# Ordering the mixers' weight copies behind the product two blocks back

## The chip, the cores and the metric

The kernel runs on one core of a Trainium2 chip. Each engine of the core (TensorE, called PE in the profile, with its weight loads as PEld; VectorE, DVE; ScalarE, ACT; GpSimd, POOL; and SyncE, SP, which here only issues transfers) works through its own list of instructions in the order in which the list was written, and semaphores hold an instruction back until what it needs is there. The metric is the time of one execution on the device, in microseconds (us).

## The reference

An input of 512 tokens of 1024 features goes through a first block (one layer) and then a second block of two layers, each of which is a feed-forward part, a hybrid mixer and another feed-forward part. The change touches the two mixers alone:

```python
for l in range(DEPTH_2):                       # 2
    x = layer_norm(DN_ALPHA * x + 0.5 * swiglu(x, ffn1_w1[l], ffn1_w3[l], ffn1_w2[l]), ...)
    y = hybrid_mixer(x, w_in[l], ...)
    x = layer_norm(DN_ALPHA * x + y, ...)
    x = layer_norm(DN_ALPHA * x + 0.5 * swiglu(x, ffn2_w1[l], ffn2_w3[l], ffn2_w2[l]), ...)

def hybrid_mixer(x, w_in, ...):
    h = split_columns(x @ w_in)
    y_a = mla_mixer(...)            # latent attention
    y_b = nsa_mixer(...)            # compressed, selected and windowed attention
    y_c = dsa_mixer(...)            # attention to the top k keys of an index score
    y_d = stick_breaking_mixer(...)
    y = concatenate([y_a, y_b, y_c, y_d]).reshape(B, S, 4, D_GROUP)
    return rms_norm_2(y, group_norm_g).reshape(B, S, D_MIX) @ w_out
```

## The kernel before

Everything is kept transposed: features on the partitions, 512 tokens along the free axis. A product of float32 values is made of three passes in the `fp32r` type: each operand is split into a high part (rounded) and a low part (the rest), and hi·hi, hi·lo and lo·hi are accumulated in PSUM. Activations are split once; the weights are split on the fly by `wstream`. It loads two blocks of weights at a time into a raw buffer `wraw` (two of them) by a transfer on SP's queue, writes the high part `whi` on ACT (`copy_a`, L363; in the output projection, whose weights are centred first, L447) and the low part `wlo` on DVE (L455, or L448 when centred) or, for the two streams named in `LO_POOL` (cq and ckv), on POOL (L367). There are three buffers each of `whi` and `wlo`, so a copy can run up to three blocks ahead of the product that reads it, and waits for PE to be done with the block that had the buffer before.

`gemm_blocks` runs a product block by block: three passes over each of the 8 pieces of the contraction (kt = 8, 24 matmuls of 512 columns) into one PSUM tile, then an epilogue `epi` that takes it out. The output projection w_out is done as four products of kt = 2, one for each group of 256 features, as the groups come ready. `gemm_m_blocks` does the token-major products (p_tok, p_sv), whose epilogue is a COPY on DVE (L1280).

What the mixer does, in order: `lead` makes four projections at once (index queries iq, misc, cmp); p_tok; the DSA index scores with p_sq, p_sk and p_sv beside them; `compress` (rows gt, with a memset on POOL, transfers on SP and a COPY on DVE each); the stick-breaking attention with p_ckv, p_cq, p_nq, p_nk and p_dq beside it; then three rounds of softmax attention (`attend`) with the pieces of w_out beside them. Rotary embeddings (`rope`: a shuffle into yc, yc times sin and the sum on DVE, hz times cos on POOL) follow several projections. The top k of the index scores is a long row of MAX8 and MATCH_REPLACE instructions on DVE, spread over the stick-breaking part. Once a group's attention is done, `group_norm` squares it on ACT, adds the halves on DVE (L1340, ss) and sums with a matmul of ones.

The order of the instructions on every engine is not written by hand: a scheduler takes the program, simulates a timeline, and emits the lists. The weight copies stand under `high_priority()`, so they are put as early as their inputs and their buffers allow. `_dep(later, earlier)` tells the scheduler that one instruction comes after another, without a semaphore of its own.

Of the kernel before, what the change touches and what calls it, by code (L numbers as in the profile page):

```python
# [13 lines left out]
AF = mybir.ActivationFunctionType  # L14
# [9 lines left out]
KT = D // 128  # L24
# [273 lines left out]
class Builder:  # L298
# [9 lines left out]
    def __init__(self, ctx, tc, A, out, dbg=None, stop=None):  # L308
        self.ctx, self.tc, self.nc, self.A, self.out = ctx, tc, tc.nc, A, out
        self.dbg = dbg or {}  # L310
        self.stop = stop
        self.n = 0
        self.set = None
        self.group, self.barrier = [], None


    def uid(self, s):
# [42 lines left out]
        return i  # L360

    def copy_a(self, out, in_):
        self.nc.scalar.activation(out, in_, AF.Copy)  # L363

    def add_p(self, out, a, b, op=ALU.add):

# [43 lines left out]
    def wstream(self, name, nhalf, F, lo_pool=False, center=False, tag=None, alt=()):  # L410

        src = self.A[name]
        nc = self.nc
        per = RAW // F
        kt = F // 128
        done = 0
        while done < nhalf:
            n = min(per, nhalf - done)  # L420
            raw = self.t("wraw", (128, RAW))
            off = done * 128 * F
            nc.sync.dma_start(raw[:, :n * F], src[off:off + n * 128 * F].rearrange("(p f) -> p f", p=128))
            if center:
                rm = self.t("rm", (128, kt))
                for k in range(kt):
                    nc.vector.reduce_sum(rm[:, k:k + 1], raw.rearrange("p (m k c) -> p k m c", k=kt, c=128)[:, k],
                                         axis=AX.XY)
                nc.vector.tensor_scalar(rm, rm, -1.0 / (128 * nhalf), None, ALU.mult)
            i = 0  # L430
            while i < n:
                t = "PT" if done + i in alt else tag
                size = 512 if t else 1024
                m = max(1, min(size // F, n - i))
                pieces = []
                for o in range(0, m * F, size):
                    r = raw[:, i * F + o:i * F + min(o + size, m * F)]
                    hi, lo = (self.t(u, (128, size), F32R)[:, :r.shape[1]] for u in ((t, t) if t else ("whi", "wlo")))
                    pieces.append((hi, lo))
                    with self.tc.high_priority():  # L440
                        if center:
                            def blk(x):
                                return x.rearrange("p (m k c) -> p m k c", k=kt, c=128)

                            for k in range(kt):
                                rk, hk = blk(r)[:, :, k], blk(hi)[:, :, k]
                                nc.scalar.activation(hk, rk, AF.Identity, bias=rm[:, k:k + 1])  # L447
                                nc.vector.scalar_tensor_tensor(blk(lo)[:, :, k], rk, rm[:, k:k + 1],  # L448
                                                               hk.bitcast(F32), ALU.add, ALU.subtract)
                        else:  # L450
                            self.copy_a(hi, r)
                            if lo_pool:
                                self.add_p(lo, r, hi.bitcast(F32), ALU.subtract)
                            else:
                                nc.vector.tensor_tensor(lo, r, hi.bitcast(F32), ALU.subtract)  # L455
                for j in range(m):
                    yield pieces if m == 1 else [tuple(x[:, j * F:(j + 1) * F] for x in pieces[0])]
                i += m
            done += n

    @staticmethod
    def cut(pieces, c=128):
# [24 lines left out]
    def gemm_blocks(self, name, nblk, xs, epi, lead=0, lo_pool=False, center=False, hold=0, st=None):  # L487

        kt = len(xs)
        st = st or self.wstream(name, nblk, kt * 128, lo_pool, center, alt=(3,) if lead > 3 else ())
        if lead:
            self.lead([(self.cut(next(st)), lambda ps, m=m: epi(m, ps)) for m in range(lead)], xs)
            yield
        for m in range(lead, nblk):
            w = self.cut(next(st))
            ps = self.p("mm")
            for k in range(kt):
                b = self.passes(ps, w, k, xs[k], slice(0, S), kt)  # L500
                if k == 0 and m >= nblk - hold:
                    self._dep(b, self.tail)
            epi(m, ps)
            yield

    def gemm_halves(self, name, xs, epi, between, center):
# [15 lines left out]
    def gemm_m_blocks(self, name, ncol, xs, epi, lo_pool=False):  # L522

        st = self.wstream(name, ncol // 256 * 2, 1024, lo_pool)
        for c in range(ncol // 256):
            w = self.cut(next(st), 256) + self.cut(next(st), 256)
            for tt in range(NT):
                ps = self.p("mm")
                o = ps[:, :256]
                cs = slice(tt * 128, tt * 128 + 128)  # L530
                for k, (hi, lo) in enumerate(w):
                    self.mm(o, xs[k][0][:, cs], hi, k == 0, False)
                    self.mm(o, xs[k][1][:, cs], hi, False, False)
                    self.mm(o, xs[k][0][:, cs], lo, False, k == KT - 1)
                epi(c, tt, o)
                if tt % 2:
                    yield

# [711 lines left out]
    def mixers(self, l, hl, xs, norm, last):  # L1250
        nc = self.nc

        def keep(res, scale=1.0, ropes=()):
            def epi(ps):
                z = self.t("hz")
                nc.scalar.activation(z, ps, AF.Copy, scale=scale)
                res.append(z)
                if ropes:
                    self.rope(z, *ropes)

            return epi

# [7 lines left out]
        for res, name, nblk, ropes, alt in ((iq, "iq", 2, [(32, whole)], ()), (misc, "misc", 1, [(64, low), (32, up)], ()),  # L1270
                                            (cmp, "cmp", 1, [(64, low)], (0,))):
            epi = keep(res, 1.0, ropes)
            jobs += [(self.cut(w), epi) for w in self.wstream(f"p_{name}_{l}", nblk, KT * 128, alt=alt)]
        self.lead(jobs, hl)
        misc = misc[0]
        tok = [self.t("hz") for _ in range(NT)]

        def epi_tok(off):
            def epi(c, tt, ps):
                nc.vector.tensor_copy(tok[tt][:, off:off + 256], ps)  # L1280
            return epi

        self.gemm_m(f"p_tok_{l}", 256, hl, epi_tok(0))
# [15 lines left out]
        def out_part(n, first, res, hold=0):  # L1299
            def epi(m, ps):  # L1300
                x = xs[m]
                if first:
                    nc.vector.scalar_tensor_tensor(x, x, DN_ALPHA, ps, ALU.mult, ALU.add)
                else:
                    nc.vector.tensor_tensor(x, x, ps, ALU.add)

            return self.gemm_blocks(f"w_out_{l}_{n}", KT, res, epi, center=True, hold=hold)

# [15 lines left out]
        interleave(last)  # L1324
        parts[1]()
        interleave(out_part(1, False, res1, HOLD))
        n = self.Norm(self, *norm)
        self.last_product(f"w_out_{l}_2", xs, res, n)
        return n
# [368 lines left out]
```

## Time and the profile before

| | us |
|---|---|
| median of 3 runs | 3313.14 |
| lowest and highest | 3311.83, 3313.3 |
| the profiled execution, its own time | 3313.87 |
| span of that execution in the trace | 3312.1 |
| PE busy | 3206.3 (97%) |
| DVE busy | 1660.5 (50%) |
| ACT busy | 1245.8 (38%) |
| POOL busy | 426.7 (13%) |

The shares are means over the whole program. In the trace, mixer 0 lies at about 1415 to 1790 us and mixer 1 at about 2540 to 2915 us; the rest is mostly dense products.

### The profile page before, as it was taken

To read this page: it belongs to the slowest core of one execution; us is meant where nothing else is said; L and a number is where in the kernel's file an instruction comes from. 1 tells how busy PE (TensorE), PEld (TensorE's weight loads), DVE (VectorE), ACT (ScalarE), POOL (GpSimd) and SP (SyncE) were. 2 spreads that over 40 slices of the span, in tenths; PEclk is the share of its full clock that TensorE was granted. 3 is DMA by queue.
4 is the path that set the end of the run, shared out by engine and by line. 5 is a ranking of instruction groups with operands and counts; after the bars stand their busy time and mean duration, and the time that the engine had idled before them with its cause. 6 is when DMAs were issued, how large, how long until landed. Compare 5 with 4: busy or idle time off the path is not lost.

```text
span 3312.1 us, 41186 instructions
## 1 busy us (share of the span) xinstructions
PE 3206.3 (97%) x16366; PEld 2622.8 (79%) x16366; DVE 1660.5 (50%) x2795; ACT 1245.8 (38%) x2229; POOL 426.7 (13%) x509
## 2 busy tenths in 40 slices
PE   8999999999999999999799999999999998999998
PEld 7798787888888888887567888888888875688887
DVE  4244444553334333468966333453336789553335
ACT  3354624442222322245465222242223445642223
POOL 0001010210000000131433000120002315320002
PEclk9999999999999999999899999999999998999999
DMA  4221222322222222222010222212222310012221
GB/s 136 80 84 68 90 89 91 108 98 93 98 95 97 89 91 100 102 74 92 30 39 27 89 90 102 102 64 102 102 91 100 98 45 26 27 59 94 102 102 64
DMA packets 53071, 275.58 MB, mean 83 GB/s; under 512 B 11136, under 2 KB 16144, under 8 KB 22416
## 3 DMA queue, kind: packets, MB, share of 16 engines
q1 hardware_dynamic: 52736, 272.83, 23.3%
q8 instruction: 129, 2.11, 0.3%
q14 instruction: 62, 0.51, 0.0%
q10 hardware_dynamic: 144, 0.12, 0.0%
HBM read 267.69 MB, written 2.10 MB: 81 GB/s over the span
## 4 chain that ended last, share of the span: by engine, by line
PE 87%; DVE 6%; ACT 3%; POOL 1%; DMA 1%; issue 1%; SPq 0%; ACTq 0%; POOLq 0%; DVEq 0%
PE mm L370 73%; PE S L370 5%; PE T L370 4%; PE O L370 3%; PE T L939 1%; DVE wlo L455 1%; POOL x L630 1%; DVE x L586 1%; DMA wraw<-ffn_w 1%; ACT whi L363 1%; DVE yc L1245 1%; DVE x L620 0%; ACT L344 0%; DVE yc L1243 0%; DVE gt L448 0%
## 5 line engine op out<-in xcount | busy, mean ns | idle before, releaser
L370 PE MATMUL mm<-ahl,whi 128*128 128x512 f32 (+1 forms) x5104 | 1550.2, 383 | 19.6 <-DVE ahl L634 7.6
L370 PEld LDWEIGHTS mm<-ahl,whi 128*128 128x128 f32 x5104 | 943.8, 189 | 214.9 <-issue 11.1
L363 ACT ACTIVATE whi<-wraw 128x1024 fp32r<-128x1024 f32 (+1 forms) x457 | 481.9, 1056 | 1497.4 <-PE mm L370 1402.5
L370 PE MATMUL mm<-ahl,wlo 128*128 128x512 f32 (+1 forms) x2552 | 971.4, 382 | 0.2
L455 DVE TENSOR_TENSOR wlo<-wraw,whi 128x1024 fp32r<-128x1024 f32 (+1 forms) x451 | 573.6, 1273 | 665.3 <-ACT whi L363 657.0
L370 PE MATMUL mm<-hz,whi 128*128 128x512 f32 x1792 | 560.2, 394 | 1.3 <-DVE x L1175 1.3
L370 PEld LDWEIGHTS mm<-ahl,wlo 128*128 128x128 f32 x2552 | 481.5, 189 | 94.6 <-DVE wlo L455 2.8
L370 PEld LDWEIGHTS mm<-hz,whi 128*128 128x128 f32 x1792 | 336.2, 188 | 81.2 <-DVE x L1175 3.0
L370 PE MATMUL mm<-hz,wlo 128*128 128x512 f32 x896 | 352.3, 394 | 0.0
L574 POOL TENSOR_TENSOR ss<-x,x 128x512 f32<-128x512 f32 x6 | 8.7, 1456 | 1564.4 <-DVE x L1175 1564.4
L370 PEld LDWEIGHTS mm<-hz,wlo 128*128 128x128 f32 x896 | 168.1, 188 | 39.8
L370 PE MATMUL mm<-whi,ahl 128*128 128x256 f32 x896 | 170.1, 289 | 7.3 <-DVE hz L1280 6.4
L1157 DVE SCALAR_TENSOR_TENSOR tA<-mm,tA 128x512 f32<-128x512 f32 x80 | 55.3, 691 | 242.9 <-PE mm L370 242.9
L370 PEld LDWEIGHTS mm<-whi,ahl 128*128 128x128 f32 x896 | 143.2, 194 | 11.8 <-DVE hz L1280 6.8
L370 PE MATMUL mm<-wlo,ahl 128*128 128x256 f32 x448 | 128.2, 287 | 1.5 <-DVE wlo L455 1.5
L1175 DVE TENSOR_TENSOR x<-x,mm 128x512 f32<-128x512 f32 x64 | 43.5, 685 | 140.4 <-PE mm L370 140.1
L363 ACT ACTIVATE hz<-tA 128x512 fp32r<-128x512 f32 (+1 forms) x124 | 76.0, 617 | 48.7 <-DVE tA L800 40.6
L374 DVE TENSOR_TENSOR hz<-tA,hz 128x512 fp32r<-128x512 f32 (+1 forms) x124 | 82.4, 669 | 20.2 <-ACT hz L363 19.7
L370 PE MATMUL O<-PT,hz 128*64 128x128 f32 (+2 forms) x776 | 87.7, 287 | 2.2 <-ACT PT L363 2.2
L363 ACT ACTIVATE PT<-T 128x128 f32<-128x128 f32 (+3 forms) x146 | 63.8, 442 | 67.3 <-PE T L939 62.7
L370 PEld LDWEIGHTS mm<-wlo,ahl 128*128 128x128 f32 x448 | 86.9, 194 | 2.6 <-DVE wlo L455 2.1
L924 DVE TENSOR_REDUCE sm<-S 128x1 f32<-128x256 f32 (+3 forms) x128 | 61.5, 488 | 42.2 <-PE S L370 30.8
(351 smaller groups left out, 3627.6 us busy)
## 6 DMA issues: line engine op xcount, KB each, us to landing
wraw<-ffn_w SPq DMA_DIRECT2D x132, 1024.0 KB, 4.8
wraw<-w_gate SPq DMA_DIRECT2D x16, 1024.0 KB, 4.8
wraw<-w_up SPq DMA_DIRECT2D x16, 1024.0 KB, 4.8
wraw<-w_dn SPq DMA_DIRECT2D x16, 1024.0 KB, 4.8
wraw<-w_br SPq DMA_DIRECT2D x8, 1024.0 KB, 4.8
wraw<-w_out SPq DMA_DIRECT2D x8, 1024.0 KB, 4.7
wraw<-w_o SPq DMA_DIRECT2D x4, 768.0 KB, 4.9
gt<-PT SPq DMA_DIRECT2D x48, 64.0 KB, 2.0
```

What stands on the lines that cost most here:

```text
L363: self.nc.scalar.activation(out, in_, AF.Copy)
L370: return self.nc.tensor.matmul(out, lhsT, rhs, start=start, stop=stop, skip_group_check=True)
L374: self.nc.vector.tensor_tensor(lo, src, hi.bitcast(F32), ALU.subtract)
L455: nc.vector.tensor_tensor(lo, r, hi.bitcast(F32), ALU.subtract)
L574: i = nc.gpsimd.tensor_tensor(s1, xs[0], xs[1], ALU.add)
L586: nc.vector.tensor_tensor(xs[d], xs[d], m0, ALU.subtract)
L630: nc.gpsimd.tensor_scalar(y, y, 1.0, be, ALU.mult, ALU.add)
L924: nc.vector.reduce_max(st[:, 0:1], ps, axis=AX.X, negate=True)
L939: nc.tensor.transpose(pt[:, j * 128:j * 128 + 128], P[:, j * 128:j * 128 + 128], self.ident)
L1157: nc.vector.scalar_tensor_tensor(s, ps, 0.5, s, ALU.mult, ALU.mult)
L1175: nc.vector.tensor_tensor(x, x, ps, ALU.add)
L1245: nc.vector.tensor_tensor(xr[r], xr[r], self.c2(f"sin{dim}")[r], ALU.mult)
```

## The change

A list `ends` is opened in each mixer after `lead`, and closed before the last piece of w_out. Every product appends the instruction of its epilogue (of the token-major products each second one). `paced` then makes the copy of a weight's high part on ACT depend on the entry two back in the list for products with kt = 8, six back for w_out. It is an ordering alone: no instruction is added or taken out, and no instruction waits for a semaphore that it didn't need anyway.

```diff
--- before.py
+++ after.py
@@ -312,6 +312,7 @@
         self.n = 0
         self.set = None
         self.group, self.barrier = [], None
+        self.ends = None
 
 
     def uid(self, s):
@@ -360,7 +361,7 @@
         return i
 
     def copy_a(self, out, in_):
-        self.nc.scalar.activation(out, in_, AF.Copy)
+        return self.nc.scalar.activation(out, in_, AF.Copy)
 
     def add_p(self, out, a, b, op=ALU.add):
 
@@ -444,11 +445,11 @@
 
                             for k in range(kt):
                                 rk, hk = blk(r)[:, :, k], blk(hi)[:, :, k]
-                                nc.scalar.activation(hk, rk, AF.Identity, bias=rm[:, k:k + 1])
+                                self.paced(nc.scalar.activation(hk, rk, AF.Identity, bias=rm[:, k:k + 1]), kt)
                                 nc.vector.scalar_tensor_tensor(blk(lo)[:, :, k], rk, rm[:, k:k + 1],
                                                                hk.bitcast(F32), ALU.add, ALU.subtract)
                         else:
-                            self.copy_a(hi, r)
+                            self.paced(self.copy_a(hi, r), kt)
                             if lo_pool:
                                 self.add_p(lo, r, hi.bitcast(F32), ALU.subtract)
                             else:
@@ -457,6 +458,12 @@
                     yield pieces if m == 1 else [tuple(x[:, j * F:(j + 1) * F] for x in pieces[0])]
                 i += m
             done += n
+
+    def paced(self, i, kt):
+
+        back = 2 if kt == KT else 6
+        if self.ends is not None and len(self.ends) >= back:
+            self._dep(i, self.ends[-back])
 
     @staticmethod
     def cut(pieces, c=128):
@@ -500,7 +507,9 @@
                 b = self.passes(ps, w, k, xs[k], slice(0, S), kt)
                 if k == 0 and m >= nblk - hold:
                     self._dep(b, self.tail)
-            epi(m, ps)
+            end = epi(m, ps)
+            if self.ends is not None:
+                self.ends.append(end)
             yield
 
     def gemm_halves(self, name, xs, epi, between, center):
@@ -532,7 +541,9 @@
                     self.mm(o, xs[k][0][:, cs], hi, k == 0, False)
                     self.mm(o, xs[k][1][:, cs], hi, False, False)
                     self.mm(o, xs[k][0][:, cs], lo, False, k == KT - 1)
-                epi(c, tt, o)
+                end = epi(c, tt, o)
+                if self.ends is not None and tt % 2:
+                    self.ends.append(end)
                 if tt % 2:
                     yield
 
@@ -1253,10 +1264,11 @@
         def keep(res, scale=1.0, ropes=()):
             def epi(ps):
                 z = self.t("hz")
-                nc.scalar.activation(z, ps, AF.Copy, scale=scale)
+                end = nc.scalar.activation(z, ps, AF.Copy, scale=scale)
                 res.append(z)
                 if ropes:
                     self.rope(z, *ropes)
+                return end
 
             return epi
 
@@ -1272,12 +1284,13 @@
             epi = keep(res, 1.0, ropes)
             jobs += [(self.cut(w), epi) for w in self.wstream(f"p_{name}_{l}", nblk, KT * 128, alt=alt)]
         self.lead(jobs, hl)
+        self.ends = []
         misc = misc[0]
         tok = [self.t("hz") for _ in range(NT)]
 
         def epi_tok(off):
             def epi(c, tt, ps):
-                nc.vector.tensor_copy(tok[tt][:, off:off + 256], ps)
+                return nc.vector.tensor_copy(tok[tt][:, off:off + 256], ps)
             return epi
 
         self.gemm_m(f"p_tok_{l}", 256, hl, epi_tok(0))
@@ -1300,9 +1313,8 @@
             def epi(m, ps):
                 x = xs[m]
                 if first:
-                    nc.vector.scalar_tensor_tensor(x, x, DN_ALPHA, ps, ALU.mult, ALU.add)
-                else:
-                    nc.vector.tensor_tensor(x, x, ps, ALU.add)
+                    return nc.vector.scalar_tensor_tensor(x, x, DN_ALPHA, ps, ALU.mult, ALU.add)
+                return nc.vector.tensor_tensor(x, x, ps, ALU.add)
 
             return self.gemm_blocks(f"w_out_{l}_{n}", KT, res, epi, center=True, hold=hold)
 
@@ -1324,6 +1336,7 @@
         interleave(last)
         parts[1]()
         interleave(out_part(1, False, res1, HOLD))
+        self.ends = None
         n = self.Norm(self, *norm)
         self.last_product(f"w_out_{l}_2", xs, res, n)
         return n
```

The lists that come out differ on all engines, in both mixers. Three places follow; line numbers of the changed kernel are up to 13 higher.

DVE in p_tok, the stretch in which the four rotary embeddings follow `lead`. The name `mm_10826` is the first PSUM tile of p_tok, which COPY hz_10812 empties; `yc` and `hz` are the rotary embeddings, `wlo_11001` the low part of p_sq's first block. Before:

```order
L455 TENSOR_TENSOR wlo_11001<-wraw_10998,whi_11000 128x1024
L1243 STREAM_SHUFFLE yc_10798<-hz_10796 128x512
L1248 TENSOR_TENSOR hz_10782<-hz_10782,yc_10784 128x512
L1243 STREAM_SHUFFLE yc_10807<-hz_10805 128x512
L1245 TENSOR_TENSOR yc_10791<-yc_10791,c_8040 128x512
L1280 COPY hz_10812<-mm_10826 128x256
L1245 TENSOR_TENSOR yc_10798<-yc_10798,c_8040 64x512 x2
L1280 COPY hz_10813<-mm_10852 128x256
```

And in the changed kernel:

```order
L1254 STREAM_SHUFFLE yc_10807<-hz_10805 128x512
L1259 TENSOR_TENSOR hz_10782<-hz_10782,yc_10784 128x512
L1256 TENSOR_TENSOR yc_10791<-yc_10791,c_8040 128x512
L1256 TENSOR_TENSOR yc_10798<-yc_10798,c_8040 64x512 x2
L1256 TENSOR_TENSOR yc_10807<-yc_10807,c_8040 64x512
L1293 COPY hz_10812<-mm_10826 128x256
L1293 COPY hz_10813<-mm_10852 128x256
```

The low part has moved from ahead of the COPY to behind it, and two multiplications of yc_10798 and one of yc_10807 have moved ahead of it.

POOL in `compress` and at the start of the stick-breaking part: the memsets of `gt` are those of compress, `wlo_11464` is the low part of p_ckv, `wlo_11531` and `wlo_11602` those of p_cq, and tA is stick-breaking. Before:

```order
L1483 AFFINE_SELECT acc_10930<-acc_10930 128x128
L367 TENSOR_TENSOR wlo_11464<-wraw_11461,whi_11463 128x1024
L1522 MEMSET gt_11355 128x272
L1483 AFFINE_SELECT acc_10930<-acc_10930 128x128
L1522 MEMSET gt_11366 128x272
L1522 MEMSET gt_11377 128x272
L1522 MEMSET gt_11388 128x272
L367 TENSOR_TENSOR wlo_11531<-wraw_11528,whi_11530 128x1024
L367 TENSOR_TENSOR wlo_11602<-wraw_11528,whi_11601 128x1024
L1483 AFFINE_SELECT acc_10930<-acc_10930 128x128
L1662 TENSOR_SCALAR tA_11505<-PT_11502 128x128
```

And in the changed kernel (from the memset of gt_11355 on):

```order
L1535 MEMSET gt_11355 128x272
L1496 AFFINE_SELECT acc_10930<-acc_10930 128x128
L1535 MEMSET gt_11366 128x272
L368 TENSOR_TENSOR wlo_11464<-wraw_11461,whi_11463 128x1024
L1535 MEMSET gt_11377 128x272
L1535 MEMSET gt_11388 128x272
L368 TENSOR_TENSOR wlo_11531<-wraw_11528,whi_11530 128x1024
L1496 AFFINE_SELECT acc_10930<-acc_10930 128x128
L1675 TENSOR_SCALAR tA_11505<-PT_11502 128x128
```

`wlo_11464` now stands behind the memset of gt_11366; `wlo_11602` no longer stands behind `wlo_11531` but thirteen rows below it, behind tA_11772. On PE, the first scores of stick-breaking (S_11494, S_11561) now stand ahead of the last eight matmuls of compress, which before came ahead of them.

DVE ahead of the norm of the stick-breaking group: `ss_12210` is the sum for which PE's matmul waits; `wlo_12721` is the low part of the first weights of w_out's second piece, `x` the centring of the residual, `yc_12107` and `hz_12105` a rotary embedding of p_dq, `hz_13483` a split for the last attention. Before:

```order
L448 SCALAR_TENSOR_TENSOR wlo_12721<-wraw_12714,rm_12716,whi_12720 128x4x128
L1243 STREAM_SHUFFLE yc_12107<-hz_12105 128x512
L399 TENSOR_TENSOR hz_13483<-hz_10796,hz_13482 64x512
L1433 COPY gt_12143<-hz_10796 32x512
L1245 TENSOR_TENSOR yc_12107<-yc_12107,c_8040 128x512
L924 TENSOR_REDUCE sm_12231<-S_12228 128x1
L924 TENSOR_REDUCE sm_12245<-S_12242 128x1
```

with four rows of x between these and the following:

```order
L1248 TENSOR_TENSOR hz_12105<-hz_12105,yc_12107 128x512
L924 TENSOR_REDUCE sm_12281<-S_12278 128x1
L1340 TENSOR_TENSOR ss_12210<-ss_12210,ss_12212 128x512
L389 TENSOR_TENSOR hz_13488<-hz_12020,hz_13488 64x512
L931 TENSOR_SCALAR sm_12231<-sm_12231 128x1
```

And in the changed kernel, ahead of and behind the same sum:

```order
L597 TENSOR_TENSOR x_5421<-x_5421,ss_12187 128x512
L430 TENSOR_SCALAR rm_13850<-rm_13850 128x2
L1446 COPY gt_12143<-hz_10796 32x512
L1254 STREAM_SHUFFLE yc_12107<-hz_12105 128x512
L935 TENSOR_REDUCE sm_12245<-S_12242 128x1
L1353 TENSOR_TENSOR ss_12210<-ss_12210,ss_12212 128x512
L935 TENSOR_REDUCE sm_12281<-S_12278 128x1
L400 TENSOR_TENSOR hz_13483<-hz_10796,hz_13482 64x512
L942 TENSOR_SCALAR sm_12231<-sm_12231 128x1
L1256 TENSOR_TENSOR yc_12107<-yc_12107,c_8040 128x512
L390 TENSOR_TENSOR hz_13488<-hz_12020,hz_13488 64x512
L935 TENSOR_REDUCE sm_12296<-S_12293 128x1
```

Ahead of the sum both parts of wlo_12721, the multiplication of yc_12107, the addition into hz_12105 and hz_13483 are gone; the last three stand behind it, wlo_12721 far behind, among the attention.

## Rows read from the trace of the kernel before

**Rows 1.** The page: busy time of PE and DVE, and the two weight copies' groups

```profile
PE 3206.3 (97%) x16366; PEld 2622.8 (79%) x16366; DVE 1660.5 (50%) x2795; ACT 1245.8 (38%) x2229; POOL 426.7 (13%) x509
...
L363 ACT ACTIVATE whi<-wraw 128x1024 fp32r<-128x1024 f32 (+1 forms) x457 | 481.9, 1056 | 1497.4 <-PE mm L370 1402.5
...
L455 DVE TENSOR_TENSOR wlo<-wraw,whi 128x1024 fp32r<-128x1024 f32 (+1 forms) x451 | 573.6, 1273 | 665.3 <-ACT whi L363 657.0
```

**Rows 2.** Busy time by window: us, PE, PEld, DVE, ACT, POOL, granted clock, DMA

```profile
1530.00:1600.00 70.00, 70.00 (x337) 50.45 (x337) 61.23 (x148) 35.25 (x75) 11.56 (x26) 0.95 0.13 47
1600.00:1655.00 55.00, 38.02 (x142) 23.48 (x140) 51.98 (x97) 23.52 (x52) 28.45 (x23) 0.81 0.05 20
...
2732.00:2787.00 55.00, 38.55 (x150) 23.01 (x149) 52.58 (x103) 27.51 (x65) 32.00 (x27) 0.81 0.06 19
```

**Rows 3.** Waits from 1430 to 1790: total us, times, longest us

```profile
ACT whi L363 <- PE mm L370: 29.7, 12, 9.8
...
ACT whi L447 <- PE mm L370: 16.3, 5, 4.8
```

**Rows 4.** Timeline in p_tok: start, us, instruction, [idle before, releaser]

```profile
1466.39 1.21 DVE L455 TENSOR_TENSOR wlo<-wraw,whi 128x1024 fp32r<-128x1024 f32 x1
...
1470.89 0.41 DVE L1280 COPY hz<-mm 128x256 f32<-128x256 f32 x1
1471.22 3.11 DVE L1245 TENSOR_TENSOR yc<-yc,c 64x512 f32<-64x512 f32 x2
...
1471.35 0.50 PE L370 MATMUL mm<-whi,ahl 128*128 128x256 f32 x2 [3.19 <-DVE hz L1280]
...
1474.82 0.68 DVE L1245 TENSOR_TENSOR yc<-yc,c 64x512 f32<-64x512 f32 x1
```

**Rows 5.** Timelines of POOL, DVE and PE at the end of compress

```profile
1517.58 5.11 POOL L367 TENSOR_TENSOR wlo<-wraw,whi 128x1024 fp32r<-128x1024 f32 x2 [1.03 <-ACT whi L363]
...
1515.62 0.75 DVE L1480 SCALAR_TENSOR_TENSOR acc<-tA,sm,acc 128x512 f32<-128x512 f32 x1
...
1516.67 0.58 DVE L1525 COPY gt<-hz 64x128 f32<-64x128 f32 x2
...
1517.86 2.63 DVE L1480 SCALAR_TENSOR_TENSOR acc<-tA,sm,acc 128x512 f32<-128x512 f32 x1
1520.41 2.70 DVE L1525 COPY gt<-hz 64x128 f32<-64x128 f32 x2
...
1523.21 1.61 PE L370 MATMUL mm<-gt,gt 128*68 128x128 f32 x8 [2.07 <-POOL wlo L367]
```

**Rows 6.** Busy time by window behind that wait

```profile
1523.50:1537.00 13.50, 13.50 (x53) 10.60 (x50) 11.52 (x42) 5.67 (x16) 1.64 (x5) 0.50 0.13 41
```

**Rows 7.** Timelines of DVE and PE ahead of the stick-breaking group's norm

```profile
1603.60 0.75 DVE L448 SCALAR_TENSOR_TENSOR wlo<-wraw,rm,whi 128x512 fp32r<-128x512 f32 x1 [2.02 <-ACT whi L447]
...
1635.47 0.75 DVE L448 SCALAR_TENSOR_TENSOR wlo<-wraw,rm,whi 128x512 fp32r<-128x512 f32 x1
...
1636.76 0.67 DVE L399 TENSOR_TENSOR hz<-hz,hz 64x512 fp32r<-64x512 f32 x1
...
1638.86 1.64 DVE L1245 TENSOR_TENSOR yc<-yc,c 128x512 f32<-128x512 f32 x1
...
1647.10 0.68 DVE L1248 TENSOR_TENSOR hz<-hz,yc 128x512 f32<-128x512 f32 x1
...
1648.86 2.04 PE L370 MATMUL mm<-ss,ones 128*128 128x512 f32 x2 [4.79 <-DVE ss L1340]
```

**Rows 8.** Timeline of PE in the first attention round

```profile
1686.11 0.66 PE L939 MATMUL T<-ident,tA 128*128 128x128 f32 x4 [1.74 <-POOL tA L934]
```

**Rows 9.** Timelines of DVE and PE: a low part of p_nq, a top-k row, the product's first matmuls

```profile
1556.03 1.23 DVE L455 TENSOR_TENSOR wlo<-wraw,whi 128x1024 fp32r<-128x1024 f32 x1 [1.01 <-ACT whi L363]
...
1567.84 0.69 DVE L1496 MAX8 m<-acc 128x8 f32<-128x512 f32 x1
...
1572.49 0.72 PE L370 MATMUL mm<-ahl,whi 128*128 128x512 f32 x2
```

## The prediction

> **What bounds the kernel now.** I read the busy shares first [rows 1]: PE works 97% of the span, so all that an ordering can give back is time in which PE stands still or runs at half its clock, or time that PE would newly lose. The groups of the two weight copies show that a copy of a high part takes 1.06 us on ACT and waits for PE nearly always (1402.5 of its 1497.4 us of idle time), and that the low part takes 1.27 us on DVE and then waits for ACT. The copies thus run as far ahead as three buffers allow and stand in front of other work while they wait for a buffer; the reader is to see that the new ordering doesn't make a copy wait for more, it puts other instructions in front of it.
>
> Then I cut the mixers into windows [rows 2]. From 1530 to 1600 PE is busy throughout and DVE for 61.23 of 70 us. From 1600 to 1655 it turns over: DVE is busy 51.98 of 55 us and PE only 38.02, at a granted clock of 0.81; the window of mixer 1 that lies 1132 us later shows the same (52.58 and 38.55). So in this window DVE's list sets the time, and ahead of it PE does. The waits of the mixer say what the copies cost the lists they stand in [rows 3]: ACT stands 29.7 us in 12 waits, and in w_out's copies 16.3 us in 5, for a buffer that PE still reads. Idle time of ACT is worth nothing by itself; it is worth something where DVE or PE waits for what stands behind.
>
> **The change, place by place (one mixer; the second has the same order).**
>
> *p_tok: a loss.* PE waits 3.19 us here for the COPY that frees its PSUM tile [rows 4]. A low part (1.21 us) leaves DVE's list ahead of the COPY, but two multiplications of yc_10798 (3.11 us for the two, beside POOL's part of the rotary embeddings) and one of yc_10807 come ahead of it. The last took 0.68 us once POOL had gone quiet. At its worst it takes half of 3.11, so that the COPY comes 3.11 + 1.55 - 1.21 = 3.45 us later; at best all three take 0.68, and it is 2.04 - 1.21 = 0.83 us. POOL's work doesn't move much, so I take the multiplications nearer the upper price, and 2.5 us.
>
> *Compress: a gain that may not show.* PE waits 2.07 us for the last eight matmuls. The row puts it down to POOL's low part; the last thing that ended before is DVE's COPY of gt, which took 2.70 us for two where the pair before took 0.58, as an accumulation took 2.63 instead of 0.75, both beside the 5.11 us in which POOL made two low parts [rows 5]. In the changed list the second of these is far behind, and PE has scores of stick-breaking to do before it needs gt, so I expect the wait to go. Behind it the granted clock is 0.50, that is 1.2 of 2.4 GHz, for 13.5 us of unbroken work [rows 6]; at full clock these take half, 6.75 us less. The bounds are 0 and 2.07 + 6.75 = 8.8 us. I take 1: what PE wins here it mostly waits out at 1600, where DVE is late, and POOL's second low part is only moved.
> The Trainium skill ("SBUF — State Buffer", "SBUF: two separate sides") says that VectorE and GpSimd share one port pair as an exclusive lock, held for a whole instruction, and that a VectorE instruction with two SBUF inputs is blocked by it. The stretched rows agree (2.63 against 0.75 us). By that rule the moved low part would block DVE again at its new place; that is a rival below.
>
> *1600 to 1655: the main gain.* PE waits 4.79 us for the sum ss of the stick-breaking group [rows 7], and in the window as a whole PE stands 17 us, while DVE has 3 us free. Ahead of the sum the changed list lacks w_out's low part in two halves (0.75 each), the multiplication of yc (1.64), the addition into hz (0.68) and a split (0.67): 4.5 us. A wait of DVE for a w_out copy (2.02 us, the first of these rows) can go too, since copies no longer stand ahead of their turn. Lower bound: no gain, if what DVE lacks then is PE's or ACT's result, and a loss of 2.3 us if the gates of NSA hold PE up, since one rotary embedding's multiplication and addition (1.64 + 0.68) now stand ahead of them. Upper bound: the 17 us that PE stands. I take 4.5, the rows taken out and nothing else. What is late next is the rotary embedding of p_dq, needed for the last attention only.
>
> *The attention rounds.* The w_out copies come later here, among the rounds, where they no longer stand in front. A wait of PE for POOL, 1.74 us [rows 8], stands behind DVE work of this kind; I take 1.7 as gone, with 0 and 4 as bounds (the short waits beside it, and the half clock behind them, make up the rest). If the moved low parts crowd DVE in the later rounds it is a loss of 1.
>
> *Weights that come too late: nothing.* A copy may now begin when the product two blocks back has ended, and needs 1.06 + 1.27 us [rows 1] and its place in DVE's list. Before, the low part of p_nq was made at 1556.03 and read first after 1572.49 [rows 9], so 16 us of lead are there, of which the low part itself takes 1.2. The changed list puts 19 rows of the top k ahead of it, at 0.69 us at most if they are like the row of that group, 13 us. What covers it is the lead alone; if that is gone, each block waits for up to a copy of each kind, 2.3 us, and for 12 waiting copies in a mixer that would be 28 us.
>
> Sum for a mixer: +2.5 - 1 - 4.5 - 1.7 = -4.7 us; for two, -9.4. On the profiled execution's 3313.87 us that is 3304.5; the median of the runs lies 0.73 lower, so 3304 us to the nearest.
>
> **Rivals.** *The clock comes back (more gain).* If compress's stall goes and PE's earlier arrival does move DVE's list, a mixer gains 8.8 instead of 1: +2.5 - 8.8 - 4.5 - 1.7 = -12.5, and two give 3288 us. For it: the half clock begins right behind that stall. Against it: DVE is 87% busy from 1530 on.
> *Nothing measurable.* The delayed COPY and late arrivals eat what DVE's list saves: for each mixer +2.5 and -1.7, and PE's 4.79 us wait only changes its name; about 3314. For it: PE's own work after 1530 leaves little to shorten.
> *The lock moves.* The low part of p_cq (2.5 us on POOL, half of 5.11) blocks DVE at its new place, in a stretch where DVE sets the time: -4.7 + 2.5 = -2.2 for a mixer, 3309.5. For it: the two stretched rows. Against it: the rows that were stretched are of other kinds than the top k which fills DVE there.
> *Slower: p_tok's COPY decides.* It comes 3.45 us later, PE's stall of 3.19 becomes 6.6, and a half clock as long as that behind compress follows (6.75 us); 1600 to 1655 gains nothing, since DVE's inputs come later by as much. +3.45 + 6.75 - 1.7 = 8.5 for a mixer, 3330 us; without the half clock 3317. It decides from the point at which the COPY's delay passes the 4.5 us that DVE's list gives back, clock included. *Slower: late weights.* If half of the 12 copies come late by 2.3 us, a mixer loses 13.8 and wins 4.7: 3331 us.
>
> **How the numbers follow.** A change of under 0.2%, 6.6 us, is about what a measurement of this kernel can't tell from none. Chances: the forecast 0.41, the clock's return 0.15, nothing 0.16, the lock 0.07, p_tok's COPY 0.12, late weights 0.09. Faster by over 0.2% are the first two, 0.56; within it the next two, 0.23; slower the last two, 0.21, though the first of these starts within. The likeliest case alone, by its bounds, is 3295 to 3310. The range takes in the clock's return with a little of its upper bounds (two mixers at -14.5: 3284) and the milder end of p_tok's COPY, 3320; beyond it lie late weights, the COPY with half clock and a full return of all idle time at 1600.
>
> **What would show it.** In the changed trace, p_tok's PE wait for the COPY should be 5 to 6.5 us instead of 3.19. The eight matmuls at compress should start without a wait, and the 13.5 us behind at a clock near 1. ss should come some 5 us sooner after the end of the top k, and PE's window there hold less idle time. No row of PE or its weight loads should wait for wlo in the mixers. The prediction fails if such waits appear, if the COPY's delay is carried through to the end of the mixer, or if DVE's idle time before 1600 grows by what its list has lost.

## The result, and the profile after

The changed kernel is slower: a median of 3335.59 us over 6 runs (3324.84 to 3338.57) against 3313.18 for the kernel before, a recorded ratio of 1.0061 with a 95% interval of 1.0050 to 1.0073 (the two medians alone give 1.0068). The forecast was 3304 us, and the range ended at 3320. Two things are to be kept apart: where the loss came from, and why six runs of one program now lie 14 us apart, when six of before lie within 2 (and the 16 to 23 of before in the groups below within 8 to 10). One execution each of `out_only` (12050.25 us), `sq_only` (8049.49) and `tok_act` (8249.82) below lasted far longer than all others and is left out of their ratios and medians here, which moves the medians by at most 1.2 us (`sq_only`'s is 3328.21 with it).

The profiled execution is the fastest of the six, 3324.84 us, with a span of 3322.8. Of the page, the lines that answer to [rows 1]:

```profile
PE 3209.3 (97%) x16362; PEld 2620.7 (79%) x16366; DVE 1659.4 (50%) x2795; ACT 1250.0 (38%) x2229; POOL 426.5 (13%) x509
...
L364 ACT ACTIVATE whi<-wraw 128x1024 fp32r<-128x1024 f32 (+1 forms) x457 | 482.2, 1057 | 1460.5 <-PE mm L371 1368.4
...
L456 DVE TENSOR_TENSOR wlo<-wraw,whi 128x1024 fp32r<-128x1024 f32 (+1 forms) x451 | 577.4, 1281 | 672.7 <-ACT whi L364 664.6
```

Busy times hardly differ, which is right for a change of order: DVE's differs by 1 us and PE's by 3. The span grew by 10.7 us, so PE stands still (span less busy time) for 113.5 us instead of 105.8: 7.7 of the 10.7 us are PE standing longer. The windows that answer to [rows 2]:

```profile
1530.00:1600.00 70.00, 70.00 (x349) 49.95 (x350) 61.01 (x153) 36.15 (x77) 14.90 (x28) 1.00 0.11 39
1600.00:1655.00 55.00, 38.60 (x140) 22.62 (x138) 50.19 (x99) 25.07 (x56) 29.13 (x22) 0.81 0.10 39
2732.00:2787.00 55.00, 37.88 (x145) 25.07 (x145) 51.19 (x92) 22.66 (x48) 26.34 (x22) 0.85 0.11 39
```

From 1600 to 1655 PE is busy 38.6 us, where it was 38.0: the gain that the forecast rested on is not there. Of the waits of [rows 3], ACT's for a buffer of whi fell from 29.7 to 12.4 us in the mixer, and its row for w_out's copies is gone from the list. The copies wait less for a buffer, as they were meant to, but PE works no more for it.

```profile
ACT whi L364 <- PE mm L371: 12.4, 4, 9.8
```

The waits of PE in mixer 0 (1400 to 1810, in us, times, longest) name what it stood for instead:

```profile
PE T L1618 <- DVE tA L1616: 7.8, 1, 7.8
PE mm L371 <- DVE hz L1293: 6.4, 1, 6.4
PE S L371 <- ACT tA L357: 3.7, 2, 3.2
...
PE S L371 <- DVE PT L1667: 2.3, 1, 2.3
...
PE mm L371 <- DVE wlo L456: 0.3, 1, 0.3
```

The second row is p_tok's COPY, 3.19 us in [rows 4]. On the timeline of DVE and PE it reads:

```profile
1467.45 5.80 DVE L1256 TENSOR_TENSOR yc<-yc,c 128x512 f32<-128x512 f32 x4
1473.18 0.74 DVE L1293 COPY hz<-mm 128x256 f32<-128x256 f32 x2
...
1473.64 0.80 PE L371 MATMUL mm<-whi,ahl 128*128 128x256 f32 x2 [6.36 <-DVE hz L1293]
```

Four multiplications take 5.80 us ahead of the COPY, and PE stands 3.17 us longer (6.36 less 3.19). Mixer 1 has the same wait of 6.36 us, so the two make 6.3 of the 7.7 us that PE stands longer. The fourth row is new: where [rows 5] had PE wait 2.07 us for the end of compress, it now waits for DVE's first tiles of stick-breaking, in both mixers:

```profile
1528.79 0.49 PE L371 MATMUL S<-PT,c 128*128 128x128 f32 x2 [2.31 <-DVE PT L1667]
...
2654.31 0.49 PE L371 MATMUL S<-PT,c 128*128 128x128 f32 x2 [2.30 <-DVE PT L1667]
```

DVE comes late to this tile for two reasons that the trace shows. It has three more rows ahead of it than before (an accumulation, a MAX8 and a MATCH_REPLACE8 with its load), and another accumulation on the way takes 2.93 us, where the one behind it takes 0.73, beside POOL's low part of p_cq's first block. Mixer 1 has the same row (2.92 us). No run parts the two reasons.

```profile
1521.24 2.93 DVE L1493 SCALAR_TENSOR_TENSOR acc<-tA,sm,acc 128x512 f32<-128x512 f32 x1
...
1521.28 2.35 POOL L368 TENSOR_TENSOR wlo<-wraw,whi 128x1024 fp32r<-128x1024 f32 x1 [2.22 <-ACT whi L364]
```

And here the two mixers part, with one order of instructions and one and the same wait. The windows behind it:

```profile
1530.50:1554.00 23.50, 23.50 (x138) 16.33 (x138) 21.99 (x77) 13.04 (x34) 4.89 (x13) 1.00 0.01 4
...
2655.00:2678.00 23.00, 23.00 (x77) 14.93 (x78) 14.97 (x54) 9.95 (x25) 4.86 (x13) 0.50 0.00 0
```

In mixer 0 the granted clock stays at 1.00, that is 2.4 GHz, and PE gets 138 matmuls done in 23.5 us; in mixer 1 it is 0.50, 1.2 GHz, and PE does 77 in 23 us, while DVE, which is fed by PE here, is busy 15 us instead of 22. The transfer that opens each mixer dates the loss. Before and after, for the first and the second mixer:

```profile
1400.03 0.33 SPq L423 DMA_DIRECT2D wraw<-p_iq  x1
...
2526.73 0.33 SPq L423 DMA_DIRECT2D wraw<-p_iq  x1
```

```profile
1400.79 0.33 SPq L424 DMA_DIRECT2D wraw<-p_iq  x1
...
2524.30 0.33 SPq L424 DMA_DIRECT2D wraw<-p_iq  x1
```

Mixer 0 and the feed-forward parts behind it take 1123.5 us instead of 1126.7, 3.2 less; from mixer 1 to the end of the span it is 798.5 instead of 785.4, 13.1 more. So in this execution the mixer whose clock holds behind the new wait is slightly faster than before, and the one whose clock falls there loses 13 us. Of these, PE stands 5.7 us longer (48.0 against 42.3, p_tok's 3.2 among them) and works 7.4 us longer, before and after:

```profile
2526.73:3312.10 785.37, 743.08 (x3924) 594.32 (x3922) 465.55 (x913) 326.45 (x679) 167.13 (x200) 0.97 0.20 70
...
2524.30:3322.80 798.50, 750.46 (x3922) 597.65 (x3922) 466.54 (x913) 328.31 (x679) 165.74 (x200) 0.96 0.20 69
```

Over the whole program the mean granted clock is 0.984 in this run, as in the profile of before, so its loss is mostly standing time. The slower runs have a lower clock besides: 0.982 in the next (3331.18 us), and 0.979 to 0.980 in the four others (3334.84 to 3338.57). That a slower run has a long half clock in both mixers is inferred from these means; only the fastest has a profile.

### The profile page after: what moved, and what is told of

The parts are those of the page before. It is cut to its first block, busy times and chain, and to the rows that moved or that the text cites. A ratio compares the mean times of both kernels' runs of the same rounds, so it can differ in the third digit from the quotient of the medians.

```text
span 3322.8 us, 41165 instructions
## 1 busy us (share of the span) xinstructions
PE 3209.3 (97%) x16362; PEld 2620.7 (79%) x16366; DVE 1659.4 (50%) x2795; ACT 1250.0 (38%) x2229; POOL 426.5 (13%) x509
## 4 chain that ended last, share of the span: by engine, by line
PE 88%; DVE 6%; ACT 2%; DMA 1%; issue 1%; POOL 1%; SPq 0%; ACTq 0%; DVEq 0%; POOLq 0%
PE mm L371 74%; PE S L371 5%; PE T L371 4%; PE O L371 3%; PE T L950 1%; DVE wlo L456 1%; POOL x L641 1%; DMA wraw<-ffn_w 1%; DVE yc L1256 1%; DVE x L597 1%; ACT whi L364 1%; DVE x L631 0%; DVE rm L428 0%; DVE yc L1254 0%; ACT L345 0%
## 5 line engine op out<-in xcount | busy, mean ns | idle before, releaser
L371 PEld LDWEIGHTS mm<-whi,ahl 128*128 128x128 f32 x896 | 143.5, 195 | 18.1 <-DVE hz L1293 13.1
```

The source lines that it names most:

```text
L371: return self.nc.tensor.matmul(out, lhsT, rhs, start=start, stop=stop, skip_group_check=True)
```

## The experiments

Eleven kernels, each timed beside runs of the kernel before on the same chip (medians of before: 3313.96, 3313.76 and 3313.47 us in the three groups, which are close enough to compare medians between groups). They differ in which copies are ordered, or in who makes one COPY.

### Which part of the ordering costs

`prod_only` leaves w_out's copies as before, `out_only` orders them alone:

```diff
-        back = 2 if kt == KT else 6
-        if self.ends is not None and len(self.ends) >= back:
+        back = 2
+        if kt == KT and self.ends is not None and len(self.ends) >= back:   # prod_only
+        back = 6
+        if kt != KT and self.ends is not None and len(self.ends) >= back:   # out_only
```

> Only the copies of products with kt = 8 are ordered; w_out's copies stand as before. Theory (the loss is PE's longer wait for p_tok's COPY and the wait at the start of stick-breaking, each with a half clock behind it): as slow as the full change, 3325 to 3340 us, with runs 10 us apart, p_tok's wait at 6.4 us and the 2.3 us wait at the first stick-breaking tile in both mixers. Rival (w_out's copies come too late among the attention rounds): 3310 to 3316 us.

Measured: 3331.96 us, ratio 1.0051 (1.0039 to 1.0064). p_tok's wait is 6.36 us, the new wait 2.31 and 2.32 us, and the half clock follows in both mixers of this profile, for some 10 us in the first and 23 in the second (3325.52 us, so a half clock in both mixers does not by itself make a run as slow as the median). The loss is in the products' copies.

> Only w_out's copies are ordered, six blocks back; the products' copies stand as before. Theory: p_tok's wait stays 3.2 us, nothing moves before the attention rounds, and the time is 3308 to 3316 us with runs within 3 us of each other. Rival (w_out's copies come too late): 3320 us or more, with waits of PE for wlo or whi in the attention rounds.

Measured: 3316.9 us, ratio 1.0005 (0.9996 to 1.0014): no difference. PE's waits from 1600 to 1660, before:

```profile
PE mm L370 <- DVE ss L1340: 4.8, 1, 4.8
PE S L370 <- ACT tA L356: 4.1, 1, 4.1
PE S L370 <- DVE gt L1433: 4.0, 1, 4.0
```

and with w_out's copies ordered:

```profile
PE S L371 <- ACT tA L357: 9.1, 2, 5.0
PE S L371 <- DVE gt L1446: 7.0, 2, 6.0
```

The wait for ss is gone, and the other two have grown from 8.1 to 16.1 us. w_out's low part no longer stands ahead of the sum, but DVE comes no sooner to the sum: ahead of some of the copies of gt that PE needs, it stands still for the transfer of w_out's next weights, in mixer 0 and as long in mixer 1.

```profile
1636.99 2.35 DVE L428 TENSOR_REDUCE rm<-wraw 128x1 f32<-128x1024 f32 x2 [2.32 <-DMA wraw<-w_out]
```

So this run shows that the ordering of w_out's copies is worth nothing, and not what an earlier sum would be worth; that is read from the trace of the full change, in the part on why the prediction was wrong.

`after_tok` opens the list only ahead of compress, so that p_sq, p_sk and p_sv are not ordered, nor the copies of p_ckv and of p_cq's first block, which are written while the list has fewer than two entries; `not_pool` orders all but the two streams whose low parts POOL makes:

```diff
         self.lead(jobs, hl)
-        self.ends = []
...
+        self.ends = []                       # after_tok
         comp = self.compress(l, cmp[0])
...
-                            self.paced(self.copy_a(hi, r), kt)
+                            i_ = self.copy_a(hi, r)
+                            if not lo_pool:  # not_pool
+                                self.paced(i_, kt)
```

> The ordering begins only ahead of compress, so p_tok, p_sq, p_sk and p_sv have the order of before, while the low part of p_cq on POOL still moves behind the first stick-breaking rows. Theory: p_tok's wait is 3.2 us again; PE's scores of stick-breaking stand behind compress as before, so the wait at the first tile of stick-breaking is gone, and the time is 3303 to 3315 us. Rival (the moved low part on POOL blocks DVE and causes the loss): 3325 us or more in spite of p_tok.

Measured: 3297.81 us, ratio 0.9951 (0.9939 to 0.9963). This is a gain of 16 us out of the same idea, over two mixers. PE's matmuls of compress now run through, with no wait at the last eight, and the clock holds behind them. The row of PE, and the windows behind it in mixers 0 and 1:

```profile
1517.96 3.76 PE L371 MATMUL mm<-gt,gt 128*68 128x128 f32 x32
```

```profile
1518.00:1536.00 18.00, 17.06 (x114) 13.09 (x113) 17.95 (x57) 12.59 (x34) 4.77 (x11) 1.00 0.12 38
2634.00:2652.00 18.00, 17.06 (x109) 12.56 (x107) 17.95 (x60) 12.76 (x35) 4.39 (x11) 1.00 0.12 38
```

> All copies are ordered but those of the two streams whose low parts POOL makes (ckv and cq), so POOL's list is that of before, while p_tok's COPY stands late as in the full change. Theory: p_tok's wait is 6.4 us; that alone costs 3.2 us and 1.7 us of half clock in a mixer, so at least 3320 us. Rival (POOL's moved low part causes the loss): 3310 to 3316 us.

Measured: 3321.44 us, ratio 1.0025 (1.0016 to 1.0034). p_tok's wait is 6.36 us, and the time is still above before's. The rival, that POOL's moved low part is the loss, falls in this form, since the run before has p_cq's second one moved and gains. But this run is 14 us under the full change, and the intervals are apart: beside the late COPY, more than half of the loss goes when the copies of p_ckv and p_cq keep their order. PE's wait for the first tile of stick-breaking is 0.32 us here instead of 2.31 (with 1.50 at the end of compress, and half clock for 6.8 us behind).

### The COPY, and what stands behind it

`sq_only` orders the copies of p_sq alone, `from_sq` opens the list behind p_tok, `tok_act` is the full change with p_tok's COPY on ACT, and `after_tok_act` has that COPY in `after_tok`:

```diff
-                            self.paced(self.copy_a(hi, r), kt)
+                            i_ = self.copy_a(hi, r)
+                            if name.startswith("p_sq"):          # sq_only, and none in w_out
+                                self.paced(i_, kt)
...
         self.gemm_m(f"p_tok_{l}", 256, hl, epi_tok(0))
+        self.ends = []                                           # from_sq
...
+                if off == 0:                                     # tok_act, after_tok_act
+                    return nc.scalar.activation(tok[tt][:, off:off + 256], ps, AF.Copy)
                 return nc.vector.tensor_copy(tok[tt][:, off:off + 256], ps)
```

> Only the copies of p_sq are ordered, which leaves p_tok's COPY as late as in the full change and all that follows compress much as before. Theory (the late COPY is the loss): p_tok's wait is 6.4 us in both mixers, PE comes late to the first tiles of stick-breaking, and the time is 3318 to 3335 us. Rival (the loss comes from the ordering of the products behind p_sq): 3311 to 3317 us.

Measured: 3327.1 us, ratio 1.0043 (1.0030 to 1.0056). p_tok's wait is 6.36 us. One product's two copies, ordered, make more than half of the loss. They also bring 11 more rows of DVE (its short MATCH_VALUE_LOAD not counted), mostly top k, ahead of the first tile of stick-breaking, for which PE then waits 3.04 us, so this run doesn't part the COPY from that backlog.

> The ordering begins behind p_tok: the COPY stands as before, p_sk and all that follows is ordered, and PE's scores of stick-breaking stand ahead of the end of compress as in the full change. Theory: no wait of over 1.5 us between p_tok and 1600 us, no half clock there, 3293 to 3305 us. Rival (the scores ahead of compress cause the new wait and its half clock): 3320 us or more.

Measured: 3310.76 us, ratio 0.9991 (0.9983 to 1.0000): between the two forecasts, 25 us under the full change and 13 us over `after_tok`. The COPY's place is worth most of the loss, but the order of the copies of p_sk, p_sv, p_ckv and p_cq's first block, which `after_tok` leaves as before, takes back most of what that run had won. The timeline of POOL, DVE and PE shows the old trouble in the new order:

```profile
1517.24 2.35 POOL L368 TENSOR_TENSOR wlo<-wraw,whi 128x1024 fp32r<-128x1024 f32 x1 [1.28 <-ACT whi L364]
...
1517.32 2.95 DVE L1538 COPY gt<-hz 64x128 f32<-64x128 f32 x2
...
1520.37 1.06 PE L371 MATMUL mm<-gt,gt 128*68 128x128 f32 x8 [1.75 <-DVE gt L1538]
```

POOL's one low part now begins just ahead of the two copies of gt and they take 2.95 us instead of 0.58; PE waits for them, and the clock is halved behind, in both mixers:

```profile
1522.00:1532.00 10.00, 9.63 (x41) 8.11 (x41) 9.26 (x27) 5.16 (x16) 0.59 (x2) 0.50 0.13 30
2645.00:2655.00 10.00, 9.30 (x39) 7.49 (x38) 8.99 (x26) 4.96 (x15) 0.59 (x2) 0.50 0.11 25
```

In `after_tok` a low part of the same length stands at nearly the same time, but DVE has an accumulation beside it, which PE doesn't wait for:

```profile
1517.18 2.35 POOL L368 TENSOR_TENSOR wlo<-wraw,whi 128x1024 fp32r<-128x1024 f32 x1 [1.03 <-ACT whi L364]
...
1517.46 2.63 DVE L1493 SCALAR_TENSOR_TENSOR acc<-tA,sm,acc 128x512 f32<-128x512 f32 x1
1520.01 0.55 DVE L1538 COPY gt<-hz 64x128 f32<-64x128 f32 x2
```

The meeting alone does not make PE wait so long: in `cq_only` below the two copies take 2.71 us beside POOL's low part, and PE, which has 24 other matmuls of compress to do meanwhile, waits 0.18 us.

> The full change, but p_tok's COPY is made by ACT instead of DVE, so that it doesn't stand behind the rotary embeddings (same work on another engine, about 0.5 us each). Theory: p_tok's wait falls below 1.5 us, the first stick-breaking tile comes without a wait, 3285 to 3302 us. Rival (the loss lies behind p_tok and not in the COPY): 3320 us or more with the 2.3 us wait still there.

Measured: 3306.24 us, ratio 0.9979 (0.9970 to 0.9988), 29 us under the full change for p_tok's COPY made by ACT. PE's wait for that COPY, now at p_sq's first matmul, is 1.97 us (expected under 1.5), and the wait at stick-breaking's first tile is gone. The time is above the expected 3302; one wait of 1.75 us for gt, as in `from_sq`, with a half clock behind, is what the trace shows for it.

> The ordering that begins ahead of compress, with p_tok's COPY on ACT. Theory: the 3.2 us wait of the kernel before in p_tok and the 3.4 us of half clock behind it go in both mixers, so up to 4.9 us for each under the run with the ordering from compress on: 3287 to 3296 us. Rival (what PE wins in p_tok it waits out at the top k): 3296 to 3300 us.

Measured: 3295.20 us, ratio 0.9945 (0.9933 to 0.9957). PE's wait for p_tok's COPY is down to 1.3 us, but the interval overlaps with that of `after_tok`: a difference between the two isn't shown.

### One move at a time

`cq_only` and `sq_cq` order the copies of p_cq alone, and of p_sq and p_cq; `after_tok_prod` is `after_tok` without w_out:

```diff
-                            self.paced(self.copy_a(hi, r), kt)
+                            i_ = self.copy_a(hi, r)
+                            if name.startswith("p_cq"):            # cq_only
+                            if name[:4] in ("p_sq", "p_cq"):       # sq_cq
+                                self.paced(i_, kt)
...
-                                self.paced(nc.scalar.activation(hk, rk, AF.Identity, bias=rm[:, k:k + 1]), kt)
+                                nc.scalar.activation(hk, rk, AF.Identity, bias=rm[:, k:k + 1])   # all three
```

> Only the copies of p_cq are ordered: POOL's second low part moves behind the first rows of stick-breaking, p_tok and the attention rounds keep the order of before. Theory (the gain of the ordering from compress on is this one move: two copies of gt no longer blocked, no wait at the last eight matmuls of compress, no half clock behind): about 7 us in a mixer up to the end of stick-breaking, 3297 to 3303 us. Rival (that gain is eaten by DVE at 1600, and what was gained comes from w_out's copies): 3310 to 3314 us.

Measured: 3306.83 us, ratio 0.9985 (0.9976 to 0.9994). DVE has the same rows ahead of the first tiles of stick-breaking and of its norm; POOL's second low part and its high part on ACT have moved. It is worth 6.6 us by the medians (5 by the ratio), half of what the theory had: the wait of 2.07 us is 0.18, but a half clock still follows (0.52 from 1526 to 1533), and the 4.8 us wait for ss stays.

> Only the copies of p_sq and p_cq are ordered: p_tok's late COPY and POOL's move together, nothing else. Theory (the late COPY brings PE's compress up against DVE's backlog, so that the move can no longer save the clock): the wait and half clock at the start of stick-breaking stay, 3318 to 3332 us, little better than p_sq alone (3328.21). Rival (the two simply add): p_sq alone less the gain of p_cq alone, about 3314 us if that is 14 us.

Measured: 3323.74 us, ratio 1.0032 (1.0020 to 1.0043). With the COPY late, a wait of 3.02 us for the first tile of stick-breaking and the half clock stay. But by the ratios p_sq alone costs 0.43% and p_cq alone gives 0.15%, and the sum of the two, 0.28%, lies within the interval of this run; the claim that the late COPY makes the move worthless isn't borne out, only that the move doesn't make up for it.

> The ordering from compress on without w_out's copies. Theory (w_out's copies are worth nothing, as they were alone): 3295 to 3300 us, as with them (3297.81). Rival (they are worth the 1.5 us of low parts ahead of the norm and the waits of the attention rounds, 3 us in a mixer, once PE's clock is up): 3302 to 3306 us.

Measured: 3296.20 us, ratio 0.9952 (0.9939 to 0.9964), the same as with w_out's copies. Their ordering is worth nothing, here as alone.

## Why the prediction was wrong

**p_tok: right.** The step took 2.5 us between 0.83 and 3.45; the wait grew by 3.17. The step did not count the clock behind the longer wait, and little is lost by that. The half clock lasts 6.8 us instead of 3.4, but much of it falls on the wait itself: PE works 3.46 us at half clock in mixer 0 and 5.00 in mixer 1, where it worked 3.40 before. (The 1.7 us that the expectation of `not_pool` adds for it are too much for the same reason.) After, in both mixers, and before:

```profile
1470.30:1477.10 6.80, 3.46 (x16) 3.46 (x17) 6.75 (x12) 1.27 (x4) 1.61 (x2) 0.50 0.22 55
...
2596.70:2603.50 6.80, 5.00 (x23) 5.00 (x24) 6.74 (x15) 2.77 (x6) 0.14 (x1) 0.50 0.24 58
```

```profile
1472.40:1475.80 3.40, 3.40 (x18) 3.40 (x17) 3.32 (x5) 0.21 (x1) 1.38 (x1) 0.50 0.32 77
```

**Compress: the step that failed.** It said "PE has scores of stick-breaking to do before it needs gt, so I expect the wait to go", and took the clock behind it at no more than a gain that is waited out later. In the changed kernel the wait did go from compress, and stood again some matmuls on, at the tiles whose scores PE had done early: DVE was behind, with three more rows ahead of the first tile and an accumulation stretched from 0.73 to 2.93 us. The step asked what PE needed and did not ask what DVE would still have to do when PE came there. In place of a gain of 1 us stood a wait of 2.3 us, and in mixer 1 the 23 us at half clock behind it, where before had some 13.5. Its sizing failed too: `after_tok` shows that the ordering from compress on, met by an unchanged start, is worth about 8 us in a mixer (16 for two), near the step's upper bound of 8.8, of which POOL's move alone makes about 3 (`cq_only`); the step had 1. The argument that an early PE only waits at 1600 was wrong, since DVE in stick-breaking is fed by PE: at half clock DVE was busy 14.97 us of 23, at full clock 21.99 of 23.5.

**1600 to 1655: wrong, and the largest term of the sum.** The 4.5 us were read off the rows ahead of one sum. In mixer 0 that sum did come 6 us sooner, counted from the transfer that opens the mixer, and PE has no wait for it (before, then after):

```profile
1648.04 0.68 DVE L1340 TENSOR_TENSOR ss<-ss,ss 128x512 f32<-128x512 f32 x1
...
1642.74 0.68 DVE L1353 TENSOR_TENSOR ss<-ss,ss 128x512 f32<-128x512 f32 x1
```

PE is busy 38.60 us of the window all the same, where it was 38.02: other results of DVE and ACT took the sum's place, NSA's gated scores first (7.81 us for tA in mixer 0). The lower bound had named these gates, and the rival "nothing measurable" had said that PE's wait only changes its name. The wait of [rows 7] was one of several of nearly the same length, and the list behind it was not followed. In mixer 1 the sum came 13 us later than before, counted likewise.

**The attention rounds: not shown.** The 1.74 us of [rows 8] are gone in mixer 0, and a wait of 1.50 stands ten us later; w_out's ordering, to which the step ascribed them, is worth nothing in two pairs of runs.

**Late weights: right.** PE waits 0.3 us for wlo at the start of p_tok in each mixer, as it did before, and nowhere else in the mixers; the lead [rows 9] was enough.

**The rivals.** "p_tok's COPY decides" came nearest, with 3317 us without the half clock and 3330 with it, at a chance of 0.12. It placed the half clock behind p_tok and the reason for no gain at 1600 in DVE's inputs; measured, the half clock that the change adds lies mostly behind stick-breaking's first tile, in mixer 1. That the lock moves was given 0.07, and 2.5 us in a mixer; in the full change an accumulation is stretched by 2.2 us, but by p_cq's first low part and not by the second, which the rival had in mind, and in `from_sq` that part meets the copies of gt. (The rival's 3309.5 lacks the 0.73 us that the other sums take off; it would be 3308.7.)

**A mixer that came near the forecast by luck.** Mixer 0 of the profiled execution is 3.2 us shorter, where the sum had 4.7. The gains at 1600 and in the attention rounds, 6.2 us of that sum, did not come; what came instead is full clock behind compress, where before had 13.5 us at half clock [rows 6].

By differences of medians: ordering the copies from p_sq to p_cq's first block turns the 16 us gain of `after_tok` into 18 to 22 us of loss; beginning behind p_tok (`from_sq`), which restores the COPY, gives 25 back, and making the COPY on ACT 29. Leaving p_ckv and p_cq as before (`not_pool`) gives 14 back with the COPY still late, so these sizes don't simply add: the late COPY and the ordering of these two streams cost more together than each alone. Beside p_sq's copies, ordering p_cq's helps (`sq_cq`); p_ckv's by themselves were not tried, so what makes them costly together stays open. The 13 us between `from_sq` and `after_tok` lie, by the trace, at the meeting of POOL's low part with the copies of gt and the half clock behind it; that was read and not tested by itself, and which of the copies from p_sk to p_cq's first block moves that meeting was not tried.

## What to carry to other kernels

Ordering weight copies behind the work that they overtake helped here only where nothing else slipped into the place they left: list what comes ahead of each instruction that PE waits for, and price that, before counting what left. Where several results of one engine feed PE in turn, a sum over the rows ahead of one of them need be no gain. A rule of this kind is best switched on by stretch, and each stretch timed; here the same rule gives 0.5% from compress on and costs more than that from p_tok on.

## What was not expected of the hardware

A wait of 2.30 us and the same instructions behind it were followed by full clock in one mixer and by 23 us at half clock in the other, within one execution. In the profile of `prod_only` the same waits of 2.31 and 2.32 us were followed by some 10 and 23 us at half clock. What tells them apart stays open. So the median of a change that leaves PE with such waits needs several runs, and its profile shows only one of the outcomes.

A COPY of 0.58 us for two took 2.95 us when a 2.35 us instruction of POOL had begun 0.08 us earlier, and 0.55 us when it came after POOL's end; the two kernels that differ in this (`from_sq` and `after_tok`) lie 13 us apart, though not in this alone. The Trainium skill ("SBUF — State Buffer", "SBUF: two separate sides") has GpSimd and VectorE lock a shared port pair for a whole instruction. By that rule the COPY waits out POOL's instruction, and the trace agrees: 2.95 is about 2.35 + 0.58.
